# A decoder block's MLP in Strassen form: down products that share PSUM banks, and another order of the up products

## Chip, cores and metric

The kernel runs on one core of one Trainium2 chip. The metric is the device time of one execution in microseconds, the median over runs.

## What is computed

One pre-norm decoder block on 1024 tokens of width 1024, in float32. The change touches the MLP (and the last norm, which follows it); the attention part before it is left as it is.

```
v = rmsnorm(h, mlp_norm_g)
hid = square(relu(v @ w_up))        # 1024 x 4096
h = h + hid @ w_down                # 1024 x 1024
out = rmsnorm(h, final_norm_g)
```

## The kernel before

Each float32 operand of the MLP is split into a high part and a low part (`split2`: ScalarE casts the high part, VectorE or GpSimd subtracts it for the low one), and one product takes three matmuls (high x high, high x low, low x high). Both matrix products are done in 2 x 2 blocks by Strassen-Winograd: seven products in place of eight.

**Up** (lines 1188 to 1300). The 4096 columns of `w_up` are worked off in 16 quads. A quad forms blocks c11, c12, c21, c22 of the hidden values, each 128 x 512, by products named 1 to 7, of 12 matmuls of 128x512 each. `quads` writes the order by hand; TensorE's order is that of the program. For the first six quads products 1 and 2 are done earlier, and the order is (6, 5, 7, 3, 4); then it is (1, 6, 5, 7, 2, 3, 4). The last two quads run as a pair, product by product. Products and banks: 1 then 2 into `a`; 6 into `b`; 5 into `d`, and 3 on top of it; 7 into `c`, and 4 on top of it. Between them VectorE forms u2 = b + p1, u4 = d + u2 (line 1251) and c22 = c + u4 (line 1255), so product 3 enters `d` only when u4 has been read, and product 4 enters `c` only when c22 has been read. ScalarE copies p1 out of `a` before product 2 enters (line 1237). `weights(q + 1)` issues all loads, differences and splits of the next quad's weights ahead of quad q's products. After each block VectorE forms relu squared and the sums s1 to s4 that down's products want, and SyncE stores them to DRAM; the last two quads form no sums.

**Down** (line 1349 on). The 4096 rows of `w_down` are worked off in eight chunks of 512. For the first seven, `down(c)` runs seven Strassen products in the order `DORD`; each has four row blocks of 128, each block 6 matmuls (line 1395) into a PSUM tile `dn` of its own (8 tiles), and VectorE adds the tile to that product's accumulator (line 1401), seven accumulators of 128x512 by four. `prep` forms each product's operand: differences over 128x1024 in SBUF on VectorE (lines 1373, 1376, 1379, 1382) and a split. The last chunk is classical: 8 results, 192 matmuls (line 1453) after 28 combine adds of the accumulators (lines 1423 to 1429). Then come the final norm's square, mean and scale (lines 1437 to 1442) and the stores, tile by tile of 128 rows.

PSUM tiles and SBUF buffers come from pools whose next user waits for the last reader; each engine works its instructions off in order, and SyncE issues all loads and stores in order.

Of the kernel before, what the change touches and what calls it, by code (L numbers as in the profile page):

```python
# [9 lines left out]
F32 = mybir.dt.float32  # L10
# [13 lines left out]
def tile_hymba_block(  # L24
# [55 lines left out]
    def rsqrt_mean(dst, ssq, n, width, eng=None):  # L80
        m = const.tile([P, 16], F32, name="rs_mean", tag="rs_mean", bufs=3)
        (eng or nc.vector).tensor_scalar(m[:, :width], ssq, 1.0 / n, EPS, ALU.mult, ALU.add)  # L82
        nc.gpsimd.tensor_tensor(dst, m[:, :width], mhalf[:, :width], ALU.pow)  # L83
# [1024 lines left out]
    def store_hid(q, v, ap):  # L1108
        c, u = divmod(q, 2)
        if c < NQ // 2 - 1:  # L1110
            held.append((hv_dram[c][:, v, u], ap))
        elif v < V_S1 or v == V_A21:
            f_, th = {V_A11: (0, 0), V_A21: (0, 1), V_A12: (1, 0), V_A22: (1, 1)}[v]
            held.append((hl_dram[:, 2 * u + f_, th * 512:(th + 1) * 512], ap))
# [73 lines left out]
    def quad_w(q, pre):  # L1188
        raw = s8([P, ND, 2 * P], F32)
        for u in range(2):  # L1190
            nc.sync.dma_start(raw[:, u * HD:u * HD + HD],
                              w_up[u * 512:(u + 1) * 512, q * 2 * P:(q + 1) * 2 * P].rearrange("(k p) f -> p k f", p=P))
        r11, r12, r21, r22 = [raw[:, HD * d:HD * d + HD, f_ * P:f_ * P + P] for f_ in range(2) for d in range(2)]
        w = {}
        if not pre:
# [3 lines left out]
            w[V_A11], w[V_A12] = x[:, 0], x[:, 1]  # L1199
        a22 = raw_pool.tile([P, 2, HD, P], F32R, name="a22", tag="raw")  # L1200
# [11 lines left out]
        return w  # L1212

    ws_, st = {}, {}

    def weights(q):
        pre = q < NPRE
        ws_[q], st[q] = quad_w(q, pre), {}
        if pre:
            c, u = divmod(q, 2)  # L1220
            a11 = o2_tile("ho")
            nc.sync.dma_start(a11[:], hv_dram[c][:, V_A11, u])
            st[q]["p1"], st[q]["c11"] = p1_of[q][0], a11

    def quads(qs, order):
        def step(what, q):
# [6 lines left out]
            if what == 1:  # L1233
# [3 lines left out]
                nc.scalar.copy(s_["p1"][:], s_["a"][:])  # L1237
# [20 lines left out]
            elif what == 3:  # L1258
                prod(s_["d"][:], w[V_S4], B22, False, True)
                s_["c12"] = o2_tile("ho")  # L1260
                nc.vector.tensor_add(s_["c12"][:], s_["d"][:], s_["u2"][:])
                relu2(s_["c12"][:], s_["c12"][:])
                if q >= NQ - 2:
                    store_hid(q, V_A21, s_["c12"][:])
                    return
# [9 lines left out]
            else:  # L1275
# [5 lines left out]
                if q >= NQ - 2:  # L1281
# [224 lines left out]
```

## Time and profile before

| | |
|---|---|
| median of 3 runs | 1252.36 us (1252.11 to 1253.46) |
| the profiled execution | 1253.01 us |
| its span in the trace | 1251.1 us |
| busy: TensorE, VectorE | 1164.1, 954.6 us |
| busy: ScalarE, GpSimd | 531.6, 640.7 us |
| mean granted clock of TensorE | 0.982 |

The profiled execution is 1.9 us longer than its span. Busy time is that of an engine over the whole span. In the views, PE is TensorE, DVE is VectorE, ACT is ScalarE, POOL is GpSimd, SP is SyncE; a row's brackets say how long the engine stood idle before the instruction, and what it was released by.

### The profile page before, as it was taken

The page shows a single profiled execution, that of the slowest core. Times are in us where ns is not written, and L with a number is a line of the kernel's source. Part 1 is how long each engine was busy: PE and PEld are TensorE (multiplying, and loading weights), DVE is VectorE, ACT ScalarE, POOL GpSimd, SP SyncE. Part 2 cuts the span into 40 slices and gives each one's busy share as a digit, 9 for nine tenths or more (in the row PEclk, how much of TensorE's full clock was granted, in tenths as well). Part 3 has the DMA queues.
Part 4 walks back from the last instruction along what each step waited for, and adds up shares of the span by engine and source line. Part 5 has one row for each costly group of instructions (what it writes and reads, how often), then busy time and mean ns, then how long its engine had stood idle before and what let it go on. Part 6 is the DMA issues. An engine that isn't in the chain of part 4 may idle for free. (4 is left out here: it accounts for less than half of the span.)

```text
span 1251.1 us, 15875 instructions
## 1 busy us (share of the span) xinstructions
PE 1164.1 (93%) x5448; PEld 946.6 (76%) x5448; DVE 954.6 (76%) x1302; ACT 531.6 (42%) x1078; POOL 640.7 (51%) x537
## 2 busy tenths in 40 slices
PE   9998988888799999999599999999889999999997
PEld 8887766666678888887477788777668888888875
DVE  8686499999997873564878965656386899888995
ACT  6434456666766761345422222222225333334402
POOL 3433544545643361315645654545448666668652
PEclk9999999999999999999799999999989999999999
DMA  6425734342712233674336534343658434446103
GB/s 216 130 60 183 179 80 97 77 112 48 225 46 86 68 136 135 204 249 136 130 126 206 177 122 156 123 155 129 223 193 304 153 108 167 155 166 200 53 1 135
DMA packets 100288, 176.70 MB, mean 141 GB/s; under 512 B 9072, under 2 KB 53616, under 8 KB 99440
## 3 DMA queue, kind: packets, MB, share of 16 engines
q1 hardware_dynamic: 100208, 175.70, 43.8%
q8 instruction: 43, 0.70, 0.2%
q14 instruction: 37, 0.30, 0.1%
HBM read 110.13 MB, written 52.95 MB: 130 GB/s over the span
## 5 line engine op out<-in xcount | busy, mean ns | idle before, releaser
L1395 PE MATMUL dn<-s,s 128*128 128x512 f32 x1176 | 269.9, 392 | 4.6 <-DVE ho L1278 4.3
L1395 PEld LDWEIGHTS dn<-s,s 128*128 128x128 f32 x1176 | 222.2, 189 | 52.2 <-DVE ho L1278 4.7
L1076 POOL TENSOR_TENSOR s<-s,s 128x512 fp32r<-128x512 f32 x84 | 121.4, 1462 | 113.1 <-ACT s L1075 112.9
L1076 POOL TENSOR_TENSOR s<-ar,s 128x1024 fp32r<-128x1024 f32 x49 | 131.8, 2694 | 65.2 <-ACT s L1075 65.2
L1401 DVE TENSOR_TENSOR acc<-acc,dn 128x512 f32<-128x512 f32 x184 | 117.9, 677 | 31.4 <-PE dn L1395 31.3
L1075 ACT CAST s<-s 128x512 fp32r<-128x512 f32 x84 | 49.6, 619 | 177.9 <-DMA s<-in_w_up_dram 71.0
L1075 ACT CAST s<-wr 128x1024 fp32r<-128x1024 f32 x53 | 55.6, 1052 | 146.6 <-PE dn L1395 61.0
L1082 PE MATMUL pa<-b,s 128*128 128x512 f32 x384 | 97.2, 407 | 11.8 <-ACT p L1237 4.5
L1082 PEld LDWEIGHTS pa<-b,s 128*128 128x128 f32 x384 | 74.2, 196 | 30.8 <-ACT p L1237 5.7
L542 POOL TENSOR_TENSOR b<-b,w 128x512 f32<-128x512 f32 (+2 forms) x57 | 58.0, 1018 | 60.8 <-DVE w L536 41.4
L488 PE MATMUL mm<-xh,wt 128*128 128x512 f32 x256 | 87.8, 395 | 0.0
L549 PE MATMUL tr<-zid,b 128*128 128x128 f32 x288 | 52.6, 290 | 35.1 <-DVE al L557 25.1
L549 PEld LDWEIGHTS tr<-zid,b 128*128 128x128 f32 x288 | 33.5, 143 | 57.9 <-DVE al L557 43.1
L1076 DVE TENSOR_TENSOR s<-wr,s 128x1024 fp32r<-128x1024 f32 x32 | 64.8, 2024 | 6.1 <-ACT s L1075 5.6
L1076 POOL TENSOR_TENSOR s<-wr,s 128x1024 fp32r<-128x1024 f32 x21 | 51.5, 2453 | 29.4 <-ACT s L1075 29.4
L536 DVE TENSOR_TENSOR_SCAN w<-w,zid 128x129 f32<-128x129 f32 (+1 forms) x64 | 64.7, 1014 | 1.0 <-ACT w L531 0.8
L263 PE MATMUL acc<-wt,xh 128*128 128x448 f32 (+1 forms) x256 | 62.7, 379 | 1.3 <-ACT xh L214 1.3
L1082 PE MATMUL pd<-b,s 128*128 128x512 f32 x192 | 49.5, 409 | 8.3 <-DVE u L1251 4.2
L1075 ACT CAST s<-ar 128x1024 fp32r<-128x1024 f32 x49 | 51.3, 1047 | 12.5 <-DMA ar<-hv_dram 10.7
L1082 PE MATMUL pb<-t,s 128*128 128x512 f32 x192 | 49.2, 406 | 6.8 <-ACT s L1075 6.7
L488 PEld LDWEIGHTS mm<-xh,wt 128*128 128x128 f32 x256 | 48.5, 190 | 8.3 <-issue 0.2
L263 PEld LDWEIGHTS acc<-wt,xh 128*128 128x128 f32 x256 | 47.7, 188 | 9.0 <-ACT xh L214 2.0
(349 smaller groups left out, 2800.9 us busy)
## 6 DMA issues: line engine op xcount, KB each, us to landing
ar<-hv_dram SPq DMA_DIRECT2D x49, 512.0 KB, 3.7
s<-in_w_up_dram SPq DMA_DIRECT2D x32, 512.0 KB, 4.8
wr<-in_w_down_dram SPq DMA_DIRECT2D x16, 1024.0 KB, 7.1
hv_dram<-s SPq DMA_DIRECT2D x56, 256.0 KB, 2.1
hv_dram<-ho SPq DMA_DIRECT2D x42, 256.0 KB, 2.0
wr<-in_w_in_dram SPq DMA_DIRECT2D x24, 256.0 KB, 2.9
raw<-in_w_o_dram SPq DMA_DIRECT2D x8, 512.0 KB, 3.5
ht<-h_dram SPq DMA_DIRECT2D x8, 512.0 KB, 4.2
```

Of the source, the lines that this page charges most:

```text
L263: nc.tensor.matmul(accs[t][:, :width], a[:, kk, t * P:(t + 1) * P], wts[kk][:, b, :width], start=(kk == 0 and p == 0), stop=done)
L488: nc.tensor.matmul(ps[:], wt[:, a, k % 4, :], b[:, k, tsl], start=(n == 0), stop=(n == 3 * ND - 1))
L536: nc.vector.tensor_tensor_scan(rv, rv, inject, init, ALU.mult, ALU.add)
L542: eng.tensor_mul(b[:, :n], b[:, :n], w[:, 1:n + 1])
L549: nc.tensor.transpose(tr[:, j * P:(j + 1) * P], sb_a[h, Q, C, j][:, s * P:(s + 1) * P], identf[:])
L1075: nc.scalar.copy(hi, src)
L1076: eng.tensor_sub(lo, src, f(hi))
L1082: nc.tensor.matmul(ps, w[:, a, k, :], bv[:, b, k, :], start=start and n == 0, stop=n == last, skip_group_check=True)
L1395: nc.tensor.matmul(ps[:], av[:, a, u, q * P:(q + 1) * P], bv[i][:, b, u], start=(n == 0), stop=(n == 5))
L1401: nc.vector.tensor_add(dst, dst, ps[:])
```

## The change

**Down.** All eight chunks are Strassen chunks; the classical chunk and the combine adds are gone. Products 1, 6, 5 and 3 of a row block add into one PSUM bank one after the other, 7 and 4 into a second, 2 has its own. After each product the bank, as it then stands, is added to one of four result blocks (11, 21, 22, 12), which start from the residual loaded from `h_dram`. The order is (1, 2, 6, 7, 5, 4, 3). In the last chunk each result block's square, mean, scale and store follow its last add; the first column half of a tile of the upper rows is scaled by ScalarE, in the lower rows the second, after GpSimd has multiplied it by the norm's weights; the other half is scaled on VectorE. Finished tiles are held, up to two, before they are written.

```diff
-    DORD = (1, 2, 3, 5, 7, 6, 4)
+    DORD = (1, 2, 6, 7, 5, 4, 3)
...
-    acc = {i: acc_pool.tile([P, 4, 512], F32, name=f"acc{i}") for i in (1, 2, 3, 5, 7, 6, 4)}
+    acc = {k_: acc_pool.tile([P, 4, 512], F32, name=f"acc{k_}") for k_ in (11, 21, 22, 12)}
...
+    ADD_TO = {1: 11, 2: 11, 6: 21, 7: 22, 5: 22, 4: 21, 3: 12}
...
+            if i == 6:
+                nc.vector.tensor_sub(b11, b12, b11)
+                nc.vector.tensor_sub(t2[:], b22, b11)
+            elif i == 7:
+                nc.vector.tensor_sub(b12, b22, b12)
+            elif i == 4:
+                nc.vector.tensor_sub(b21, b21, t2[:])
...
+            if c == 0 and i not in DORD[:2]:
+                with tc.issue_after(st[NQ - 1]["end"].ins):
+                    prep(i)
...
-                ps = dn_ps.tile([P, 512], F32, name="dn", tag="dn")
+                if i in (1, 2, 7):
+                    banks[i, q] = dn_ps.tile([P, 512], F32, name="dn", tag="dn")
+                ps = banks[{6: 1, 5: 1, 3: 1, 4: 7}.get(i, i), q]
...
-                        nc.tensor.matmul(ps[:], av[:, a, u, q * P:(q + 1) * P], bv[i][:, b, u], start=(n == 0), stop=(n == 5))
+                        nc.tensor.matmul(ps[:], av[:, a, u, q * P:(q + 1) * P], bv[i][:, b, u],
+                                         start=i in (1, 2, 7) and n == 0, stop=n == 5, skip_group_check=True)
...
-                if c == 0 and i in (1, 5, 6):
-                    nc.scalar.copy(dst, ps[:])
-                else:
-                    nc.vector.tensor_add(dst, dst, ps[:])
+                dst = acc[ADD_TO[i]][:, q]
+                read = nc.vector.tensor_add(dst, dst, ps[:])
+                if c == NCH - 1:
+                    if i == 2:
+                        square(q, 0, dst)
+                    elif i == 5:
+                        square(4 + q, 1, dst)
+                    elif i == 4:
+                        finish(4 + q, read, square(4 + q, 0, dst))
+                    elif i == 3:
+                        finish(q, read, square(q, 1, dst))
```

**Up.** Product 3 goes to a new bank `e`, and u4 takes the place of u2 in its sum. Product 2 comes third. The next quad's weights are issued in three steps (the load; the split of `x`, which products 1 and 2 take; the rest), the last two behind the copy of product 1 for quads from the seventh on. The last two quads form s1 to s4 as all others do.

```diff
-                prod(s_["d"][:], w[V_S4], B22, False, True)
+                prod(bank("e"), w[V_S4], B22, True, True)
                 s_["c12"] = o2_tile("ho")
-                nc.vector.tensor_add(s_["c12"][:], s_["d"][:], s_["u2"][:])
+                nc.vector.tensor_add(s_["c12"][:], s_["e"][:], s_["u4"][:])
                 relu2(s_["c12"][:], s_["c12"][:])
-                if q >= NQ - 2:
-                    store_hid(q, V_A21, s_["c12"][:])
-                    return
...
-        quads([q], (6, 5, 7, 3, 4) if q < NPRE else (1, 6, 5, 7, 2, 3, 4))
-    weights(NQ - 1)
+            quads([q], (1,))
+            with tc.issue_after(st[q]["p1_ins"].ins):
+                weights(q + 1, 2)
+            quads([q], (6, 2, 5, 7, 3, 4))
+    weights(NQ - 1, 1)
     flush()
     last2 = [NQ - 2, NQ - 1]
-    quads(last2, (1, 2))
+    quads(last2[:1], (1,))
+    with tc.issue_after(st[NQ - 2]["p1_ins"].ins):
+        weights(NQ - 1, 1)
+    quads(last2[1:], (1,))
+    quads(last2, (2,))
+    with tc.issue_after(st[NQ - 1]["p1_ins"].ins):
+        weights(NQ - 1, 1)
```

How it moves instructions is shown at three places. The first is TensorE in up, one whole quad from the seventh on; a name's letter after `p` is its bank. Before:

```order
L1082 MATMUL pa_7313<-b11_5831,s8_7170 128x512 x12
L1082 MATMUL pb_7328<-t2_6380,s8_7182 128x512 x12
L1082 MATMUL pd_7343<-t1_6381,s8_7182 128x512 x12
L1082 MATMUL pc_7358<-t3_6382,s8_7183 128x512 x12
L1082 MATMUL pa_7313<-b21_5832,s8_7170 128x512 x12
L1082 MATMUL pd_7343<-b22_6383,s8_7183 128x512 x12
L1082 MATMUL pc_7358<-t4_6384,a22_7175 128x512 x12
```

With the change:

```order
L1081 MATMUL pa_7297<-b11_5831,s8_7196 128x512 x12
L1081 MATMUL pb_7334<-t2_6380,s8_7208 128x512 x12
L1081 MATMUL pa_7297<-b21_5832,s8_7196 128x512 x12
L1081 MATMUL pd_7364<-t1_6381,s8_7208 128x512 x12
L1081 MATMUL pc_7379<-t3_6382,s8_7209 128x512 x12
L1081 MATMUL pe_7395<-b22_6383,s8_7209 128x512 x12
L1081 MATMUL pc_7379<-t4_6384,a22_7201 128x512 x12
```

Product 2 (`b21`) has moved ahead of product 5 (`t1`), and product 3 (`b22`) now fills `pe` where it added into `pd`.

The second is ScalarE at the start of the last pair; `p1` is the copy of product 1, first for quad 14 and then for quad 15, `ho` the relu of product 2, and the CASTs make high parts of quad 15's weights. Before:

```order
L1075 CAST s8_8452<-s8_8449 128x512 x2
L1241 ACTIVATE ho_8408<-pa_8335 128x512
L1075 CAST a22_8457<-s8_8449 128x512
L1075 CAST s8_8464<-s8_8449 128x512
L1237 COPY p1_8494<-pa_8481 128x512
L1075 CAST s8_8464<-s8_8449 128x512
L1075 CAST s8_8465<-s8_8449 128x512 x2
L1237 COPY p1_8509<-pa_8496 128x512
L1241 ACTIVATE ho_8523<-pa_8481 128x512
L1241 ACTIVATE ho_8538<-pa_8496 128x512
```

With the change:

```order
L1238 COPY p1_8486<-pa_8473 128x512
L1074 CAST s8_8488<-s8_8463 128x512 x2
L1238 COPY p1_8506<-pa_8493 128x512
L1074 CAST a22_8538<-s8_8463 128x512
L1074 CAST s8_8545<-s8_8463 128x512
L1242 ACTIVATE ho_8520<-pa_8473 128x512
L1074 CAST s8_8545<-s8_8463 128x512
L1074 CAST s8_8546<-s8_8463 128x512 x2
L1242 ACTIVATE ho_8535<-pa_8493 128x512
```

Only casts for `x` (s8_8488) stand between the two copies now, and all casts of quad 15 stand behind the copy for quad 14.

The third is VectorE at the end of up; L1255 reads c22 of quad 14 or 15, L1261 c12, L1278 c21, and L1373 to L1382 are down's preparations. Before:

```order
L1376 TENSOR_TENSOR wr_8545<-wr_8545 128x2x512
L1117 SCALAR_TENSOR_TENSOR ho_8645<-ho_8645 128x512
L1261 TENSOR_TENSOR ho_8660<-pd_8586,u2_8569 128x512
L1117 SCALAR_TENSOR_TENSOR ho_8660<-ho_8660 128x512
L1379 TENSOR_TENSOR wr_8545<-wr_8545 128x2x512
L1261 TENSOR_TENSOR ho_8675<-pd_8601,u2_8584 128x512
L1382 TENSOR_TENSOR wr_8545<-wr_8545 128x2x512
L1117 SCALAR_TENSOR_TENSOR ho_8675<-ho_8675 128x512
L1278 TENSOR_TENSOR ho_8690<-pc_8616,u2_8569 128x512
L1117 SCALAR_TENSOR_TENSOR ho_8690<-ho_8690 128x512
L1278 TENSOR_TENSOR ho_8705<-pc_8632,u2_8584 128x512
L1117 SCALAR_TENSOR_TENSOR ho_8705<-ho_8705 128x512
```

With the change (L1262 reads c12, L1276 c21; L1265 to L1271 and L1280 form s1, s3, s2 and s4; L1412 and L1413 are down's preparations):

```order
L1262 TENSOR_TENSOR ho_8697<-pe_8684,u4_8628 128x512
L1112 SCALAR_TENSOR_TENSOR ho_8697<-ho_8697 128x512
L1265 TENSOR_TENSOR s1_8700<-ho_8697,ho_8659 128x512
L1268 TENSOR_TENSOR s3_8702<-ho_8535,ho_8697 128x512
L1271 TENSOR_TENSOR s2_8704<-s1_8700,ho_8535 128x512
L1276 TENSOR_TENSOR ho_8718<-pc_8630,u2_8583 128x512
L1112 SCALAR_TENSOR_TENSOR ho_8718<-ho_8718 128x512
L1280 TENSOR_TENSOR s4_8721<-ho_8718,s2_8682 128x512
L1276 TENSOR_TENSOR ho_8735<-pc_8646,u2_8598 128x512
L1112 SCALAR_TENSOR_TENSOR ho_8735<-ho_8735 128x512
L1280 TENSOR_TENSOR s4_8738<-ho_8735,s2_8704 128x512
L1412 TENSOR_TENSOR wr_8559<-wr_8559 128x2x512
```

The preparations of down stand behind the last read of up, and sums for quads 14 and 15 stand between the reads.

## Rows read from the trace of the kernel before

**Rows 1.** The page's busy lines: engine, busy us (share of the span), instructions.

```profile
PE 1164.1 (93%) x5448; PEld 946.6 (76%) x5448; DVE 954.6 (76%) x1302; ACT 531.6 (42%) x1078; POOL 640.7 (51%) x537
```

**Rows 2.** Windows: busy us (instructions) of PE, PEld, DVE, ACT, POOL; granted clock, DMA share, GB/s.

```profile
648.80:653.30 4.50, 4.44 (x13) 3.51 (x14) 2.19 (x2) 0.00 (x0) 3.38 (x3) 0.62 0.77 267
928.00:932.00 4.00, 3.94 (x9) 3.14 (x10) 1.99 (x4) 0.58 (x1) 0.00 (x0) 0.50 0.65 213
1038.30:1076.60 38.30, 38.30 (x171) 31.72 (x170) 32.43 (x37) 14.05 (x15) 25.12 (x10) 1.00 0.47 151
```

**Rows 3.** TensorE's waits, 640 to 1252 us: us in total, times, longest.

```profile
PE pa L1082 <- ACT p L1237: 4.5, 1, 4.5
PE dn L1395 <- DVE ho L1278: 4.3, 1, 4.3
PE pd L1082 <- DVE u L1251: 4.2, 5, 1.5
PE pd L1082 <- ACT s L1075: 4.0, 2, 2.4
PE pc L1082 <- DVE ho L1255: 1.0, 1, 1.0
PE dn L1453 <- DVE acc L1401: 0.7, 1, 0.7
```

**Rows 4.** TensorE's timeline, classical chunk: start, us, then what ran, idle before it.

```profile
1209.01 11.06 PE L1453 MATMUL dn<-s,lhr 128*128 128x512 f32 x48
```

**Rows 5.** Groups of instructions, 925 to 1200 us: busy us, mean ns.

```profile
L1401 DVE TENSOR_TENSOR acc<-acc,dn 128x512 f32<-128x512 f32 x182 | 116.6, 677 | 31.4 <-PE dn L1395 31.3
...
L1379 DVE TENSOR_TENSOR wr<-wr 128x1024 f32<-128x1024 f32 x7 | 21.6, 3090 | 5.1 <-POOL s L1076 5.1
```

**Rows 6.** VectorE's timeline at the longest wait of up.

```profile
648.04 0.68 DVE L1251 TENSOR_TENSOR u<-pd,u 128x512 f32<-128x512 f32 x1
```

**Rows 7.** TensorE's timeline at the longest wait of up.

```profile
648.86 4.59 PE L1082 MATMUL pd<-b,s 128*128 128x512 f32 x12 [2.43 <-ACT s L1075]
```

**Rows 8.** TensorE's timeline, last pair and where up meets down.

```profile
885.64 7.54 PE L1082 MATMUL pa<-b,s 128*128 128x512 f32 x24 [4.47 <-ACT p L1237]
893.02 5.75 PE L1082 MATMUL pb<-t,s 128*128 128x512 f32 x24
...
919.34 3.05 PE L1082 MATMUL pc<-t,a 128*128 128x512 f32 x12 [0.96 <-DVE ho L1255]
...
928.06 17.12 PE L1395 MATMUL dn<-s,s 128*128 128x512 f32 x64 [4.28 <-DVE ho L1278]
```

**Rows 9.** ScalarE's timeline, start of the last pair.

```profile
884.49 0.62 ACT L1075 CAST s<-s 128x512 fp32r<-128x512 f32 x1 [4.97 <-DVE s L1203]
885.01 0.58 ACT L1237 COPY p<-pa 128x512 f32<-128x512 f32 x1
```

**Rows 10.** GpSimd's timeline, start of the last pair.

```profile
880.84 1.27 POOL L1076 TENSOR_TENSOR a<-s,a 128x512 fp32r<-128x512 f32 x1
```

**Rows 11.** VectorE's timeline, in up and at the last read of up.

```profile
644.54 1.77 DVE L1284 TENSOR_TENSOR s<-ho,s 128x512 f32<-128x512 f32 x1
...
928.65 0.68 DVE L1278 TENSOR_TENSOR ho<-pc,u 128x512 f32<-128x512 f32 x1
```

**Rows 12.** VectorE's instructions by line, 909 to 927 us: busy us, mean ns.

```profile
L1373 DVE TENSOR_TENSOR wr<-wr 128x1024 f32<-128x1024 f32 x1 | 3.3, 3309 | 0.0
L1376 DVE TENSOR_TENSOR wr<-wr 128x1024 f32<-128x1024 f32 x1 | 2.8, 2802 | 0.0
...
L1379 DVE TENSOR_TENSOR wr<-wr 128x1024 f32<-128x1024 f32 x1 | 1.2, 1217 | 0.0
L1382 DVE TENSOR_TENSOR wr<-wr 128x1024 f32<-128x1024 f32 x1 | 1.2, 1211 | 0.0
```

**Rows 13.** Timeline of all engines, the end.

```profile
1240.41 1.52 PE L1453 MATMUL dn<-s,lhr 128*128 128x512 f32 x6
...
1246.77 1.42 DVE L1442 SCALAR_TENSOR_TENSOR y<-acc,fss,gfb 128x512 f32<-128x512 f32 x2 [2.03 <-POOL fss L83]
```

More of the change, by code (lines that the diff above doesn't have):

```diff
@@ L1211, in quad_w, with weights, reload_a11 @@
             w[key] = tl[:, v]
-        return w
-    ws_, st = {}, {}
-    def weights(q):
+        yield
+    ws_, st, wgen = {}, {}, {}
+    def weights(q, steps):
         pre = q < NPRE
[L1218 to L1223, printed above, removed]
+        if q not in ws_:
+            ws_[q], st[q] = {}, {}
+            wgen[q] = quad_w(q, pre, ws_[q])
+        for _ in range(steps):
+            next(wgen[q])
+    def reload_a11(q):
+        c, u = divmod(q, 2)
+        a11 = o2_tile("ho")
+        nc.sync.dma_start(a11[:], hv_dram[c][:, V_A11, u])
+        st[q]["p1"], st[q]["c11"] = p1_of[q][0], a11
     def quads(qs, order):
@@ L1280, in step @@
                 store_hid(q, V_A12, c21[:])
[L1281 to L1282 removed]
                 s4 = o2_tile("s4")
[L1284 removed]
+                s_["end"] = nc.vector.tensor_sub(s4[:], c21[:], s_["s2"][:])
                 store_hid(q, V_S4, s4[:])
@@ L1344, in load_acc, with square @@
             for q in range(4):
-                nc.sync.dma_start(acc[i][:, q], h_dram[q + rows][:, cols:cols + 512])
-        for q in range(4):
-            nc.gpsimd.tensor_sub(acc[4][:, q], acc[4][:, q], acc[7][:, q])
+                nc.sync.dma_start(acc[k_][:, q], h_dram[q + rows][:, cols:cols + 512])
+    fin = {}
+    def square(t, dh, hx):
+        sq = nc.scalar.activation(sqj[:], hx, AF.Square, accum_out=fss[t][:, dh:dh + 1])
+        fin[t, dh] = hx
+        if dh != (t < 4):
+            nc.gpsimd.tensor_mul(hx, hx, gfb[:, halves[dh]])
+        return sq
@@ new lines, in tile_hymba_block, with finish, put @@
+    ready = []
+    def finish(t, read, sq):
+        ss = fss[t]
+        nc.gpsimd.tensor_add(ss[:, 2:3], ss[:, 0:1], ss[:, 1:2])
+        rsqrt_mean(ss[:, 3:4], ss[:, 2:3], D, 1, nc.gpsimd)
+        ready.append(t)
+        with tc.issue_after(read.ins), tc.issue_after(sq.ins):
+            while len(ready) > (2 if t != 3 else 0):
+                put(ready.pop(0))
+    def put(t):
+        ss, y = fss[t], ys[t % 4]
+        for dh in ((1, 0) if t < 4 else (0, 1)):
+            sl, hx = halves[dh], fin[t, dh]
+            if dh == (t < 4):
+                nc.vector.scalar_tensor_tensor(y[:, sl], hx, ss[:, 3:4], gfb[:, sl], ALU.mult, ALU.mult)
+            else:
+                nc.scalar.activation(y[:, sl], hx, AF.Copy, scale=ss[:, 3:4])
+            if t == 3:
+                nc.sync.dma_start(out[t * P:(t + 1) * P, sl], y[:, sl])
+        if t != 3:
+            nc.sync.dma_start(out[t * P:(t + 1) * P, :], y[:])
```

126 lines of the change are left out of this document (31 added, 95 removed).

## The prediction

> **What bounds the kernel now.** I read the busy lines first: TensorE is busy 93% of the span [rows 1]. That is an average, so the next question is which stretches hold the missing 7%, and whether the change touches them. The windows of the second matrix product answer for the long steady part: TensorE is busy for all of 38.30 us at a granted clock of 1.00 while VectorE needs 32.43 [rows 2]. There only fewer matmuls help. TensorE's waits from 640 us on then give every gap [rows 3]: seven before `pd` (4.2 + 4.0 = 8.2 us), one before `pa` (4.5), one each before `pc` (1.0) and `dn` (4.3) where the two products meet, and 0.7 at the classical chunk. What lies before the up product keeps its order on every engine, so the waits before 640 us stay.
>
> **1. Fewer matmuls.** A Strassen chunk has 7 x 4 x 6 = 168 matmuls, the classical one 8 x 4 x 6 = 192; now all eight chunks have 168, so 24 go. The classical chunk ran 48 in 11.06 us [rows 4], 0.230 each, the last one's tail included: 24 x 0.230 = **-5.5 us**. Its wait of 0.7 us for an accumulator add [rows 3] goes too, as no group of blocks claims all eight banks at once any more: **-0.7**. The 28 combine adds (20 on VectorE, 8 on GpSimd) lay beside matmuls and count for nothing. VectorE's work per steady chunk stays: 28 reads and 8 operations from SBUF to SBUF. Its cover is the 38.30 - 32.43 = 5.9 us that VectorE has left [rows 2]. A bank that is used by several products must have been read before the next one enters; but there are eight banks in both kernels, one product (four blocks of 6 matmuls, 24 x 0.230 = 5.5 us) lies between a bank's use and its next use in both, and a read takes 0.677 [rows 5]. What is new is that the reads and preparations bunch differently, so that some lag is possible at eight chunk starts. The nearest row for such a lag is the 0.7 at the classical chunk [rows 3]; met once or twice in each of eight chunks it would be +6 or +11. Rows 2 show none in a steady chunk, and the slack is the same, so I allow **+1**, with 0 and +11 as ends.
>
> **2. Up: product 3 gets a bank.** Today product 3 adds into the bank `d` that product 5 filled, and must wait until VectorE has read `u4` from it. Five of the waits name that read; the other two name a cast on ScalarE, but the `u` read at line 1251 ends at 648.72 [rows 6] and TensorE goes on at 648.86 [rows 7], so they are the same wait. All seven (8.2 us) go, since product 3 now starts a bank of its own. One came with a lower clock: the window shows 0.62 [rows 2] and the product took 4.59 us in place of 2.9 (half of 5.75 for 24, [rows 8]), another 1.7. What is late next is product 4, which enters the bank `c` that c22 was read from: that read stands one VectorE instruction behind `u4`, but product 4 starts a whole product (2.9 us) after product 3. The longest of the five plain waits was 1.5 and the longest of all 2.4 [rows 3]; each plus 0.7 for the extra read is close to or below 2.9, so little is left, 0.5 by estimate. **-8.2 - 1.7 + 0.5 = -9.4**; ends: -9.9, and -2 if the wait is only handed to product 4.
>
> **3. The start of the last pair.** Product 2 of quad 14 waited 4.47 us [rows 8] for the copy of product 1, which stood behind casts of quad 15's weights on ScalarE: a cast at 884.49, then the copy at 885.01 [rows 9]. The 24 matmuls after it took 7.54 against the 5.75 of the next 24: 4.5 + 1.8 = 6.3 us. Now only quad 15's `x` split stands behind the copy for quad 14. But product 1 of quad 15 needs it: product 1(14) takes 2.9, the copy 0.58 and the first cast 0.62 [rows 9], so that with some 0.3 for the hand-overs between engines (my estimate) TensorE stands from 2.9 to about 4.4. It stands again for the first low part, 1.27 on GpSimd [rows 10], for about 0.9 more: 2.4 us of idle time: **-3.8** at full clock; ends -4.7 (only the cast is waited for) and -2.0 (1.8 for a lower clock again).
>
> **4. Where up meets down.** Before, VectorE was about 6 us behind: product 4(15) ended near 922.3 (919.34 + 3.05), its reader c21(15) ran at 928.65 [rows 8, 11]. TensorE stood 4.3 us, another 1.0 before 4(15), and ran 64 matmuls in 17.12 us [rows 8], 2.4 over 64 x 0.230, beside a clock of 0.50 [rows 2]: 7.7 us in all. Ahead of the last reads stood four preparations of down over 128x1024; they move behind the last quad: 3.31, 2.80, 1.22 and 1.21, together 8.5 us [rows 12]. New there are eight operations over 128x512 for s1, s3, s2, s4 of quads 14 and 15, since those quads now also feed Strassen products; seven of them stand ahead of the last read. At 0.68 each (the read of 128x512 in rows 11) they are 4.8, and VectorE's lag is 6.3 - 8.5 + 4.8 = 2.6 us. I add 2 for the product that follows: the loads of down's first operands come later behind the store of c11(14), and its third product's preparation (L1412, L1413, a low split) now begins only after quad 15; and 0.6 of clock. **5.2 against 7.7: -2.5.** Ends: -4.8 (the lag and 0.3 of the rest), and +8 when the seven take 1.77 each, as one of their kind did at 644.54 [rows 11] (lag 6.3 - 8.5 + 12.4 = 10.2; with the 2 for the operands, and 2.4 and 1.0 as before, 15.6).
>
> **5. The end.** Today TensorE ends near 1241.9 (1240.41 + 1.52), the last multiplication begins at 1246.77 [rows 13] and the span ends at 1251.1. After it the chain is the same in kind: add, square, mean, scale, store, with one of the last two halves on ScalarE; but results come out late and close together (first-column and second-column halves of all eight tiles in the last chunk), and up to two are held back. **+0.7**; ends -0.5 and +2.
>
> **Sum**: -5.5 - 0.7 + 1.0 - 9.4 - 3.8 - 2.5 + 0.7 = -20.2. The profiled execution took 1253.0 us, so 1232.8; the median of the runs is 0.65 lower, 1252.36, so by it **1232.2**, which I take.
>
> **The rivals.**
> (a) *VectorE becomes the pace of down; slower.* Its 32.43 us hold 28 reads x 0.677 = 19.0; eight operations share the other 13.5, 1.7 each. Were all as long as L1373's 3.31 [rows 12], VectorE would need 45.5 us per chunk, 7.2 over TensorE: 8 x 7.2 = +57, **about 1289**. It decides from a mean of 2.7 on (19.0 + 21.8 = 40.8, 2.5 over, which times eight is the whole gain). For it: L1379's mean is 3.09 [rows 5]. Against: GpSimd has no more to do than before. Chance 0.04.
> (b) *A little lag at every chunk*: the 0.7 of [rows 3] one and a half times in each, +8.4 in place of +1, **about 1239.6**. For it: each read now feeds a result block that the next read also needs, in order on one engine. Chance 0.12.
> (c) *The up wait passes to product 4* in place of vanishing: term 2 shrinks to -2, **about 1239.6**. Against: a product lies between. Chance 0.10.
> (d) *The eight new operations are blocked by GpSimd* in the handover. 128x512 out of two tiles in SBUF took 1.77 [rows 11], where reads out of PSUM take 0.68: term 4 becomes +8, **about 1242.7**. For it: GpSimd splits down's operands just then. Chance 0.12.
> The Trainium skill, "SBUF — State Buffer", section "Who interferes with whom", says that a VectorE instruction with two SBUF inputs contends with a GpSimd instruction that reads SBUF, over a port pair that is locked for the whole instruction, and that one with at most one such input does not. Rows 11 agree with that as far as they go; by it (d) would hold for each of the eight that meets a GpSimd split, and the sum would be near 1242.7; 1232.2 has them run at the length of the reads.
> (e) *The end grows* by 4, since all eight tiles come out in the last product rounds and their stores crowd: **about 1235.5**. Chance 0.05.
> (f) *The change does not do what it says*: the order of the instructions shows the new bank and the moved casts, so 0.01, 1252.
>
> **How the numbers follow.** The forecast has 0.56: its own range is 1228 to 1236. Below 1228 lie the good ends of terms 3 to 5 (0.9 + 2.3 + 1.2 = 4.4, to 1227.8). (b), (c) and (d) reach to 1242.7, two of them together to about 1250. Leaving out (a), (f) and most pairs, the range is **1227 to 1243.5**. 0.2% (2.5 us) is about what a measurement of this kernel can tell from no change. Slower by more than that needs (a): 0.03; within it are (f), a weak (a) and three rivals at once: 0.03; faster: 0.94.
>
> **What would show it.** Right: no wait before the up product's `pe`, and under 1 us before the second use of `pc`; product 1 of quad 15 waiting some 2.4 us; under 6 us idle at the first `dn`s; windows of down with TensorE full and the clock at 1.00; the last matmul some 20 us sooner. Wrong: TensorE waiting for VectorE's reads within down by more than 1 us a chunk (a, b); waits before `pc` of up (c); s1 to s4 at 1.7 us in the handover with `dn` waiting over 8 (d); more than 11 us from the last matmul to the end (e).

## The result, and the profile after

The changed kernel takes 1235.84 us (median of 4 runs, 1234.46 to 1236.29) against 1252.23 us for the kernel before: ratio 0.9866, 95% interval 0.9849 to 0.9884. That is 16.4 us faster where 20.2 were forecast (1232.2), inside the range of 1227 to 1243.5. The profiled execution took 1236.29 us with a span of 1234.5. Among the experiments' runs, one of bank_only (2187.85 us, mean clock 0.89) and one of down_only (1618.05 us, 0.65) fell into a slower state; the ratios and intervals leave them out.

TensorE's waits from 640 us on, in the trace of the changed kernel (us in total, times, longest):

```profile
PE dn L1437 <- DVE s L1075: 2.3, 1, 2.3
PE dn L1437 <- DVE ho L1276: 2.1, 1, 2.1
PE pc L1081 <- DVE ho L1256: 1.7, 2, 1.3
PE pa L1081 <- ACT s L1074: 1.2, 1, 1.2
PE pa L1081 <- POOL s L1075: 0.6, 1, 0.6
```

Against [rows 3] the seven waits before `pd` are gone, and two before the second use of `pc` have come, 1.7 us together. The start of the last pair waits 1.2 + 0.6 us where it waited 4.5, and the handover 2.3 + 2.1 where it waited 4.3 + 1.0. No wait is left inside down. TensorE's timeline at these places:

```profile
651.15 3.07 PE L1081 MATMUL pc<-t,a 128*128 128x512 f32 x12 [0.40 <-DVE ho L1256]
...
708.68 3.06 PE L1081 MATMUL pc<-t,a 128*128 128x512 f32 x12 [1.26 <-DVE ho L1256]
...
871.31 0.73 PE L1081 MATMUL pa<-b,s 128*128 128x512 f32 x2 [1.19 <-ACT s L1074]
872.66 9.62 PE L1081 MATMUL pa<-b,s 128*128 128x512 f32 x34 [0.62 <-POOL s L1075]
...
913.66 11.63 PE L1437 MATMUL dn<-s,s 128*128 128x512 f32 x43 [2.10 <-DVE ho L1276]
927.57 32.71 PE L1437 MATMUL dn<-s,s 128*128 128x512 f32 x136 [2.28 <-DVE s L1075]
```

The 34 matmuls behind the pair's wait took 9.62 us, 1.8 more than 34 x 0.230 [rows 4]. Windows over them and over the two stretches behind the waits of the handover show the granted clock, and a window over a steady stretch of down shows whether VectorE has become the pace (busy us of PE, PEld, DVE, ACT, POOL, then the clock):

```profile
872.60:882.10 9.50, 9.44 (x34) 7.62 (x35) 2.68 (x3) 2.22 (x4) 3.87 (x5) 0.82 0.00 0
914.00:928.00 14.00, 11.72 (x44) 9.27 (x43) 12.75 (x15) 5.89 (x6) 6.33 (x3) 0.87 0.94 308
928.00:932.00 4.00, 4.00 (x13) 3.11 (x13) 4.00 (x6) 0.00 (x0) 4.00 (x2) 0.63 1.05 403
1036.60:1074.90 38.30, 38.30 (x171) 31.71 (x170) 34.19 (x37) 14.03 (x14) 25.48 (x11) 1.00 0.47 151
```

The clock was 0.82 at the pair, where 1.00 was forecast, and 0.87 and 0.63 behind the two waits of the handover: means of stretches at full clock and at half, the lower of its two levels (0.50 from 873 to 876 us). In steady down TensorE is full at 1.00 as in [rows 2], with VectorE at 34.19 us of 38.30 (32.43 before), the same to 0.01 us in six such windows. The window is a little longer than a chunk: it touches 171 matmuls and not 168, and the chunks from the second on begin 38.08 us apart.

Where the time went, by stretches of the two traces (TensorE's timeline: from the span's start to the wait before the first quad's product 6, to the first matmul of the last pair, to the pair's product 6, to the first of down's second chunk, to the last of down, to the end; in the changed kernel they start at 0, 623.21, 867.22, 882.12, 956.26, 1222.98 us):

| stretch | before | after | difference | forecast |
|---|---|---|---|---|
| ahead of up's first product 6 | 621.77 | 623.21 | +1.44 | 0 |
| up to the last pair | 253.66 | 244.01 | -9.65 | -9.4 |
| products 1 and 2 of the pair | 17.59 | 14.90 | -2.69 | -3.8 |
| rest of the pair, handover, down's first chunk | 74.21 | 74.14 | -0.07 | -2.5 |
| down from its second chunk on | 274.70 | 266.72 | -7.98 | -5.2 |
| from the last matmul to the end | 9.17 | 11.52 | +2.35 | +0.7 |
| sum (span) | 1251.1 | 1234.5 | -16.6 | -20.2 |

The two rows of down make -8.05 where -7.7 was forecast, but neither does by itself. The first row is not the change's: the order of instructions there is the same in both. Over the 14 profiled executions of this study it lies between 621.25 and 624.73 us.

What made the end longer can be read in the timeline of all engines:

```profile
1210.78 2.40 POOL L1075 TENSOR_TENSOR s<-wr,s 128x1024 fp32r<-128x1024 f32 x1
...
1213.15 5.04 POOL L1368 TENSOR_TENSOR acc<-acc,gfb 128x512 f32<-128x512 f32 x4
...
1216.22 0.69 DVE L1441 TENSOR_TENSOR acc<-acc,dn 128x512 f32<-128x512 f32 x1 [0.67 <-PE dn L1437]
...
1219.29 0.75 DVE L1387 SCALAR_TENSOR_TENSOR y<-acc,fss,gfb 128x512 f32<-128x512 f32 x1 [2.39 <-POOL fss L83]
...
1219.96 0.68 DVE L1441 TENSOR_TENSOR acc<-acc,dn 128x512 f32<-128x512 f32 x1
1220.12 9.11 SPq L1393 DMA_DIRECT2D out_dram<-y  x7
```

GpSimd multiplies four halves by the norm's weights (L1368) in 5.04 us, from 1213.15, when its last split (L1075) is done. The row scale of the first finished tile stands behind that. VectorE's first scaling (L1387) waits 2.39 us for it, and the adds that read the last banks stand behind VectorE's wait: the one that should follow 1216.22 by 1.36 us comes at 1219.96. The first store is issued at 1220.12, and seven of them take SyncE 9.11 us. From the first store to the end of the span there are 14.4 us, here as in tail_split, load_one and load_four below, so that the end is as long as the first store is late. VectorE at the handover:

```profile
907.85 0.69 DVE L1265 TENSOR_TENSOR s<-ho 128x512 f32<-128x512 f32 x1
...
909.66 0.68 DVE L1262 TENSOR_TENSOR ho<-pe,u 128x512 f32<-128x512 f32 x1
...
912.92 0.68 DVE L1276 TENSOR_TENSOR ho<-pc,u 128x512 f32<-128x512 f32 x1
...
922.13 1.35 DVE L1441 TENSOR_TENSOR acc<-acc,dn 128x512 f32<-128x512 f32 x2 [0.89 <-DMA acc<-h_dram]
...
924.90 2.61 DVE L1075 TENSOR_TENSOR s<-t,s 128x1024 fp32r<-128x1024 f32 x1
```

The sums (`s`) run at 0.69 us each, between the reads of `pe` and `pc`. c21 of quad 14 is read at 912.92 only, when TensorE has stood since its first block; reads of `dn` then wait 0.89 us for their result block's load, and the low split for product 6, TensorE's second wait, comes at 924.90. GpSimd had nothing to do meanwhile:

```profile
921.67 2.42 POOL L1075 TENSOR_TENSOR s<-ar,s 128x1024 fp32r<-128x1024 f32 x1 [17.06 <-ACT s L1074]
```

### The profile page after: what moved, and what is told of

The parts are those of the page before. It is cut to its first block, busy times and chain, and to the rows that moved or that the text cites. A ratio compares the mean times of both kernels' runs of the same rounds, so it can differ in the third digit from the quotient of the medians.

```text
span 1234.5 us, 15926 instructions
## 1 busy us (share of the span) xinstructions
PE 1155.6 (94%) x5424; PEld 941.7 (76%) x5424; DVE 958.0 (78%) x1310; ACT 535.5 (43%) x1080; POOL 647.2 (52%) x539
## 5 line engine op out<-in xcount | busy, mean ns | idle before, releaser
L1437 PE MATMUL dn<-s,s 128*128 128x512 f32 x1344 | 308.6, 392 | 4.4 <-DVE s L1075 2.3
L1437 PEld LDWEIGHTS dn<-s,s 128*128 128x128 f32 x1344 | 254.4, 189 | 58.4 <-DVE s L1075 2.7
L1075 POOL TENSOR_TENSOR s<-ar,s 128x1024 fp32r<-128x1024 f32 x56 | 147.8, 2641 | 80.8 <-ACT s L1074 80.8
L1075 POOL TENSOR_TENSOR s<-s,s 128x512 fp32r<-128x512 f32 x84 | 117.0, 1414 | 109.8 <-ACT s L1074 109.8
L1441 DVE TENSOR_TENSOR acc<-acc,dn 128x512 f32<-128x512 f32 x224 | 144.0, 678 | 33.8 <-PE dn L1437 32.8
L1074 ACT CAST s<-wr 128x1024 fp32r<-128x1024 f32 x48 | 50.4, 1051 | 150.1 <-PE dn L1437 105.3
L1075 POOL TENSOR_TENSOR s<-wr,s 128x1024 fp32r<-128x1024 f32 x24 | 57.8, 2409 | 32.8 <-ACT s L1074 32.8
L1074 ACT CAST s<-ar 128x1024 fp32r<-128x1024 f32 x56 | 58.6, 1047 | 9.2 <-DMA ar<-hv_dram 9.2
L1075 DVE TENSOR_TENSOR s<-wr,s 128x1024 fp32r<-128x1024 f32 x24 | 52.4, 2182 | 6.8 <-ACT s L1074 6.8
L1112 DVE SCALAR_TENSOR_TENSOR ho<-ho 128x512 f32<-128x512 f32 x48 | 51.7, 1076 | 1.4
```

Source lines behind the costliest of these rows:

```text
L1074: nc.scalar.copy(hi, src)
L1075: eng.tensor_sub(lo, src, f(hi))
L1112: nc.vector.scalar_tensor_tensor(dst, src, 0.0, src, ALU.max, ALU.mult)
L1437: nc.tensor.matmul(ps[:], av[:, a, u, q * P:(q + 1) * P], bv[i][:, b, u], start=i in (1, 2, 7) and n == 0, stop=n == 5, skip_group_check=True)
L1441: read = nc.vector.tensor_add(dst, dst, ps[:])
```

## The experiments

Twelve kernels, in four groups, each group on its own chip beside runs of the kernel before. So the ratio to that is the number to compare; the changed kernel's is 0.9866 [0.9849, 0.9884].

| kernel | median us | ratio | interval |
|---|---|---|---|
| bank_only | 1248.27 | 0.9967 | 0.9957 to 0.9977 |
| no_bank | 1238.34 | 0.9894 | 0.9879 to 0.9909 |
| down_only | 1246.88 | 0.9955 | 0.9943 to 0.9968 |
| tail_split | 1233.49 | 0.9853 | 0.9838 to 0.9867 |
| pair_early | 1231.90 | 0.9828 | 0.9813 to 0.9842 |
| no_sums | 1229.16 | 0.9810 | 0.9794 to 0.9827 |
| load_one | 1239.51 | 0.9890 | 0.9875 to 0.9905 |
| load_four | 1263.18 | 1.0079 | 1.0064 to 1.0094 |
| old_order | 1234.17 | 0.9858 | 0.9835 to 0.9881 |
| pool_sums | 1234.84 | 0.9865 | 0.9844 to 0.9885 |
| all_three | 1231.09 | 0.9833 | 0.9818 to 0.9847 |
| loads_first | 1223.93 | 0.9763 | 0.9750 to 0.9777 |

**bank_only**, on the kernel before:

```diff
-                prod(s_["d"][:], w[V_S4], B22, False, True)
+                prod(bank("e"), w[V_S4], B22, True, True)
...
-                nc.vector.tensor_add(s_["c12"][:], s_["d"][:], s_["u2"][:])
+                nc.vector.tensor_add(s_["c12"][:], s_["e"][:], s_["u4"][:])
```

> The kernel before with one edit: product 3 of up starts a bank of its own and u4 takes the place of u2 in its sum. Everything else, the order (1, 6, 5, 7, 2, 3, 4) among it, stays. Theory (the wait was for the read of u4 out of product 3's bank): the seven waits before product 3, 8.2 us and 1.7 us of lower clock beside one of them, go; product 4 keeps at most 2 us of waits for c22. 8 to 10 us faster than before, about 1243.5. Rival (the wait is handed on to product 4, which needs the read that follows u4's): the waits before the second use of the bank c come to 6 us or more and the time falls by 3 us at most. Second rival (the new order of products does the work, not the bank): no change by the bank alone.

Measured: 0.33% faster, some 4 us: half of the theory's 8 to 10, and neither rival. TensorE's timeline shows why:

```profile
650.56 3.06 PE L1082 MATMUL pc<-t,a 128*128 128x512 f32 x12 [0.36 <-DVE ho L1255]
...
799.42 3.01 PE L1082 MATMUL pa<-b,s 128*128 128x512 f32 x12 [0.75 <-ACT p L1237]
...
861.08 3.01 PE L1082 MATMUL pa<-b,s 128*128 128x512 f32 x12 [0.99 <-ACT p L1237]
```

No product 3 waits, and product 4 waits 0.36 us in one quad of the first six. But in four later quads product 2 now waits 0.58 to 0.99 us for ScalarE's copy of product 1, which stands behind a cast for the next quad:

```profile
798.26 0.62 ACT L1075 CAST s<-s 128x512 fp32r<-128x512 f32 x1 [5.01 <-DVE s L1203]
798.78 0.58 ACT L1237 COPY p<-pa 128x512 f32<-128x512 f32 x1
```

The trace of before has no such wait; as I read it, the quads were held up at product 3 first. Up to the last pair it takes 246.59 us by its trace, 7.1 less than before, and products 1 and 2 of the pair take 19.57 us, 2.0 more: 1.0 of that are new waits at the pair's start. The bank removes all seven waits, but it uncovers the copy.

**no_bank**, the reverse edit on the changed kernel.

> The changed kernel with product 3 of up back on product 5's bank (and u2 in its sum); the new order of the products stays. Theory: the waits for u4 come back, 7 to 10 us slower than the changed kernel, about 1244.5. Rival (the new order, which puts product 2 earlier, has removed the waits): no more than 2 us slower.

Measured: ratio 0.9894 against 0.9866, 2.5 us by the medians; the intervals touch. By the trace, up to the last pair takes 248.81 us, 4.8 more than in the changed kernel, nearly all of it in two of the first six quads:

```profile
649.95 4.58 PE L1081 MATMUL pd<-b,s 128*128 128x512 f32 x12 [2.51 <-DVE u L1252]
...
710.21 3.04 PE L1081 MATMUL pd<-b,s 128*128 128x512 f32 x12 [1.92 <-DVE u L1252]
```

The run's time shows less of it, in part because the pair's lower clock stayed away here, 1.6 us (see the last section). From the seventh quad on no product 3 waits, although it adds into product 5's bank. In the first six, where the next quad's splits are issued behind product 6, the waits come back. So my term 2 came out by two causes: the bank removed the two long waits of the first six quads, and for the five short ones the reordered and split work was enough by itself.

**old_order** undoes only the place of product 2:

```diff
-            quads([q], (6, 2, 5, 7, 3, 4))
+            quads([q], (6, 5, 7, 2, 3, 4))
```

> The changed kernel with the old order of products (1, 6, 5, 7, 2, 3, 4) for the quads from the seventh on; product 3's own bank and the weights in steps behind the copy of product 1 stay. Theory, as it now stands: from the seventh quad on any of two things ends the waits for u4 (a bank of its own, or two products between 5 and 3 together with the casts behind the copy), and with the bank alone the copy of product 1 was the next thing late, since casts stood ahead of it; with the casts behind the copy the old order has no wait, so no change, within 2 us. Rival (the order itself is needed): waits of 0.6 to 1 us before product 2 in four or five quads, or before product 3, 3 us or more slower.

Measured: 0.9858 [0.9835, 0.9881], no change, and its trace has no wait before product 2. With the bank there, the new order of the products adds nothing that can be measured; what bank_only lacked is that the casts stand behind the copy of product 1.

**down_only** puts up back as a whole (product 3 on bank `d`, the old order, `weights(q + 1, 3)` ahead of each quad, `quads(last2, (1, 2))`) and keeps down and the sums.

> The changed kernel with up as before: product 3 on product 5's bank, the old order, each quad's weights issued in one piece ahead of the quad before it, both products 1 of the last pair behind all casts of quad 15. What is left of the change is down, its end and the sums of the last two quads. Theory: up costs 9.7 us more and the start of the last pair 2.7 us more than in the changed kernel, so about 1248, 4 us faster than before: 24 matmuls (-5.5) and the classical chunk's wait (-0.7) and 1 at the handover, less 2.3 for the longer end. Rival (the equal chunks alone make most of the gain): 1242 or less. Rival (down alone costs, its gain being eaten by the end and the handover): 1252 or more.

Measured: 0.9955, 5.7 us faster by the medians; 4 were expected.

```profile
885.59 8.55 PE L1081 MATMUL pa<-b,s 128*128 128x512 f32 x24 [4.53 <-ACT p L1238]
...
925.17 8.68 PE L1423 MATMUL dn<-s,s 128*128 128x512 f32 x37 [0.31 <-DVE ho L1276]
...
937.01 23.21 PE L1423 MATMUL dn<-s,s 128*128 128x512 f32 x89 [3.15 <-DVE s L1075]
```

The pair's wait for the copy is back at 4.53 us. Down, from its first matmul to its last, takes 311.60 us against 319.71, and the end is 11.53 us, as in the changed kernel. The 8.1 us were not won at the handover: the first chunk takes 44.88 us (45.01 before), and from the second chunk on there are 266.72 us, as in the changed kernel, against 274.70. At the pace of a steady chunk, 168 matmuls in 38.08 us, the 24 matmuls are 5.4 of these 8.0; the classical chunk lost another 1.6 (it takes 45.31 us, the changed kernel's last one 38.24), and two of the seven chunks before it 0.9 (38.35 and 38.71 us). The end gives 2.4 back. What the changed kernel has beyond this, 11 us by the ratios, is up: -9.8 up to the last pair and -3.7 in its products 1 and 2 by the traces, +1.4 in down's first chunk, and +1.6 ahead of up, where nothing differs.

**tail_split**, on the changed kernel:

```diff
-                        5: (b11, nc.vector), 4: (b21, nc.gpsimd), 3: (b22, nc.gpsimd)}[i]
+                        5: (b11, nc.vector), 4: (b21, nc.gpsimd),
+                        3: (b22, nc.vector if c == NCH - 1 else nc.gpsimd)}[i]
```

> The changed kernel with one edit: in the last chunk the low part of product 3's operand is subtracted on VectorE and not on GpSimd. Theory: the end is 2.3 us longer than before because GpSimd reaches its four multiplications by the norm's weights (5.04 us) and the first row scale behind them only after that split, VectorE waits 2.39 us for that scale with the reads of the last product behind it; with 2.4 us of split gone from GpSimd the scales come 2.4 us earlier, the wait goes, and the time falls by 1.5 to 2.5 us, to about 1234. Rival (the end is bound by 4 MB of stores that move at some 390 GB/s from their first issue): it gains the same only if the first store moves as early; if the first store is issued as late as now, no change. Rival (VectorE is late with the split itself): TensorE waits before product 3 of the last chunk, up to 2 us slower.

Measured: 0.9853; its interval and the changed kernel's overlap, so the ratio alone doesn't show the gain. By its trace the end takes 10.14 us after the last matmul in place of 11.52:

```profile
1209.97 5.05 POOL L1368 TENSOR_TENSOR acc<-acc,gfb 128x512 f32<-128x512 f32 x4
...
1216.93 9.11 SPq L1393 DMA_DIRECT2D out_dram<-y  x7
```

The multiplications begin at 1209.97, 11.19 us ahead of its last matmul's end (1221.16); in the changed kernel 1213.15 is 9.83 us ahead of 1222.98. They come 1.36 us earlier, and the end is 1.38 us shorter. The first store goes out 4.2 us ahead of the last matmul's end and not 2.9. The 2.4 us of the theory did not come in full: GpSimd's other split for product 3 took 3.40 us there, beside VectorE's, in place of 2.40.

**pair_early**, on the changed kernel:

```diff
+    weights(NQ - 1, 1)
     quads(last2[:1], (1,))
-    with tc.issue_after(st[NQ - 2]["p1_ins"].ins):
-        weights(NQ - 1, 1)
     quads(last2[1:], (1,))
```

> The changed kernel with one edit: the split of quad 15's x is issued before product 1 of quad 14 and not behind its copy; all other casts of quad 15 stay behind the copies. Theory: TensorE stands 1.19 and 0.62 us at the start of the last pair because product 1 of quad 15 waits for casts behind that copy, and the next 34 matmuls take 1.9 us too long at a clock of 0.82; with the split done early there is no wait, the clock stays at 1.00, and the pair starts 3.7 us faster, about 1232. Rival (the lower clock there does not come from the wait): only 1.8 us faster, 1234. Rival (the early casts delay the copy of product 1, as before the change): a wait of 2 us or more before product 2 of quad 14, no gain.

Measured: 0.9828, 0.38% below the changed kernel's ratio, 4 to 5 us.

```profile
867.06 11.06 PE L1081 MATMUL pa<-b,s 128*128 128x512 f32 x48
877.96 5.79 PE L1081 MATMUL pb<-t,s 128*128 128x512 f32 x24
```

Products 1 and 2 of the pair, 48 matmuls, take 10.90 us without a wait (14.90 in the changed kernel), and the clock stays at 1.00. The trouble before the change was that the copy stood behind casts of quad 15's sums and differences, for which ScalarE stood 4.97 us [rows 9]; the casts for `x` alone, ahead of it, delay nothing.

**no_sums**, on the changed kernel: in the last two quads `store_hid(q, v, s_["c12"][:])` for each of the four sums, and no sum formed; down's first differences follow the last relu of c21.

> The changed kernel with the eight sums s1 to s4 of quads 14 and 15 left out; c12 is stored in their places, so down's last chunk multiplies other values. Theory (VectorE's lag at the handover is made by these eight operations, 0.68 us each, 5.4 in all): the wait of 2.10 us for c21 goes, and the wait of 2.28 for the low part of product 6's operand shrinks or goes, since that part is formed 5.4 us earlier: 3 to 6 us faster than the changed kernel, about 1231.5. Rival (the wait for product 6 hangs on the loads of the result blocks or on the order of the reads, not on VectorE's lag): at most 2 us faster. Rival (GpSimd blocks these sums): they would take 1.7 us each in the changed kernel; its trace already shows 0.68, so nothing is expected of this.

Measured: 0.9810, 7 us below the changed kernel by ratio. Down's only wait is

```profile
927.72 262.55 PE L1443 MATMUL dn<-s,s 128*128 128x512 f32 x1157 [1.13 <-POOL s L1075]
```

and the low split for product 6 is

```profile
919.54 1.22 DVE L1075 TENSOR_TENSOR s<-t,s 128x1024 fp32r<-128x1024 f32 x1
```

Down takes 306.64 us from its first matmul to its last, 6.3 less than in the changed kernel; all of it is in the first chunk (39.92 us against 46.24, where a steady one takes 38.08). So most of the handover's loss in the changed kernel, waits and lower clock, comes from these eight operations of 0.69 us, by VectorE's order or by the stores that wait for them. Part of it is indirect: the split above took 2.61 us in the changed kernel, beside one that GpSimd began at 924.05. Another 1.6 of the 7 us is the pair's clock, which was not lowered in this run. The sums run at full speed in the changed kernel; rival (d) did not occur, since GpSimd stood idle for 17.06 us just there.

**load_one** and **load_four**, on the changed kernel, with `LOADS = (7,)` and `LOADS = (2, 7, 5, 3)`:

```diff
+            if i in LOADS:
+                nc.vector.tensor_sub(xtra[:], wr[:, 0], wr[:, 1])
```

> The changed kernel with one more VectorE operation in each chunk of down: the difference of two rows of 128x1024 in SBUF, written to a tile that nobody reads. Theory (TensorE paces down, VectorE has 38.30 - 34.19 = 4.1 us to spare per chunk): 1.2 to 3.3 us fit into that, no change, within 2 us. Rival (reads out of the shared banks have no slack, so that any delay of VectorE's shows): 1.2 us or more in each of eight chunks, 10 us slower or more.

> The changed kernel with four more such VectorE operations in each chunk of down, spread over products 2, 7, 5 and 3. Theory: 34.19 + 4 x 1.2 to 4 x 2.4 = 39 to 44 us per chunk against 38.3, so VectorE paces down: 5 to 45 us slower, 1241 to 1281. Rival (they fit, since the steady chunk's VectorE time holds much waiting for GpSimd that would move): under 3 us slower. It prices how near VectorE is to being the pace.

Measured: 0.9890 and 1.0079, 3 us and 27 us slower. A window of about one chunk of each, load_one first:

```profile
1036.60:1074.90 38.30, 38.30 (x171) 31.72 (x170) 35.17 (x38) 14.05 (x14) 25.77 (x11) 1.00 0.46 151
```

```profile
1057.50:1098.90 41.40, 39.27 (x168) 31.20 (x168) 41.40 (x41) 14.04 (x14) 29.21 (x11) 1.00 0.42 139
```

With one more operation TensorE stays full (VectorE at 35.17 of 38.30), and down from its second chunk on takes 266.72 us, the same as in the changed kernel: reads out of shared banks have slack. The 3 us come from elsewhere. The first chunk takes 1.5 us more, the pair's clock, not lowered in this run, gives 1.6 back, and the end is 14.3 us long, 2.8 more than in the changed kernel:

```profile
1216.14 5.04 POOL L1370 TENSOR_TENSOR acc<-acc,gfb 128x512 f32<-128x512 f32 x4
...
1222.27 0.75 DVE L1389 SCALAR_TENSOR_TENSOR y<-acc,fss,gfb 128x512 f32<-128x512 f32 x1 [5.14 <-POOL fss L83]
```

GpSimd's multiplications begin 7.06 us ahead of the last matmul's end (1223.20), 2.77 later than the 9.83 of the changed kernel, and VectorE's first scaling waits 5.14 us for the scale behind them. In load_four they begin 6.3 us ahead, 3.5 later, and the end is 15.0 us, 3.5 more. With tail_split this makes four points on one line: the end moves by what the multiplications move. With four more operations VectorE is busy for all of the 41.40 us, and the chunks begin some 41.4 us apart in place of 38.08: 3.4 us in each, 27 in eight. So what rival (a) describes begins at some 4 us more of VectorE time per chunk, and the changed kernel stays short of it.

**pool_sums**, on the changed kernel: `se = nc.gpsimd if q >= NQ - 2 else nc.vector` forms s1 to s4, and down's first differences follow the last relu of c21.

> The changed kernel with the eight sums s1 to s4 of quads 14 and 15 formed on GpSimd, which stands idle for 17 us at that place; down's first differences are issued behind the last relu of c21. Nothing is left out. Theory (the handover's waits come from these eight operations standing ahead of other work on VectorE): both waits, 2.10 and 2.28, go as where the sums were left out, 4 to 6.5 us faster than the changed kernel, about 1230.5. Rival (VectorE's operations from SBUF to SBUF, the relus and L1412, L1413, are held up by GpSimd's, and GpSimd's next splits come late): at most 2 us faster, with VectorE's 128x512 relus at 1.5 us or more.

Measured: 0.9865, no change. It is the rival's number without the rival's reason. The wait for c21 is gone; TensorE, VectorE and SyncE show the new one:

```profile
926.46 0.76 PE L1438 MATMUL dn<-s,s 128*128 128x512 f32 x1 [3.57 <-DVE acc L1442]
```

```profile
912.73 1.05 DVE L1278 SCALAR_TENSOR_TENSOR ho<-ho 128x512 f32<-128x512 f32 x1
...
915.41 2.31 DVE L1413 TENSOR_TENSOR wr<-wr 128x1024 f32<-128x1024 f32 x1
...
925.63 1.34 DVE L1442 TENSOR_TENSOR acc<-acc,dn 128x512 f32<-128x512 f32 x2 [5.69 <-DMA acc<-h_dram]
```

```profile
910.30 8.89 SPq L1105 DMA_DIRECT2D hv_dram<-s  x6
...
921.53 0.88 SPq L1361 DMA_DIRECT2D acc<-h_dram  x2
```

Beside GpSimd's sums VectorE's relus take 1.05 us in place of 0.69, and the difference over 128x1024 (L1413) 2.31, where it takes 1.22 in the changed kernel with GpSimd idle. The Trainium skill, "SBUF — State Buffer", section "Who interferes with whom", says that a VectorE instruction with two inputs in SBUF contends with a GpSimd instruction that reads SBUF; these rows agree. That loss is small here. But VectorE's first read of `dn` stands 5.69 us for the loads of the result block. SyncE issues these from 921.53 on, behind the stores of the sums, six of which hold it for 8.89 us. The sums had two followers, VectorE's reads and SyncE's queue; only one was freed.

**all_three** joins tail_split, pair_early and pool_sums.

> The changed kernel with three edits together: product 3's split of the last chunk on VectorE (2.3 us faster alone), quad 15's x split ahead of product 1 of quad 14 (4 us faster alone), and the sums of quads 14 and 15 on GpSimd (4 to 6.5 expected). They lie in three places, so they should add: 10 to 13 us faster than the changed kernel, about 1224. Rival (a lower clock that one of them removed shows up at another wait, so they don't add): 1228 or more.

Measured: 0.9833, some 4 us below the changed kernel and not the 10 to 13 us that were hoped for: no better than pair_early alone. The rival's number came, not its reason: what pool_sums paid at the handover by itself is here too, a wait of 3.70 us for VectorE's reads and a granted clock of 0.51 from 921 to 928 us, so that it adds nothing.

**loads_first**, on all_three: the stores of the last two quads are issued behind the first result block's loads.

```diff
-    flush()
...
-                nc.sync.dma_start(acc[k_][:, q], h_dram[q + rows][:, cols:cols + 512])
+                ld = nc.sync.dma_start(acc[k_][:, q], h_dram[q + rows][:, cols:cols + 512])
+            if k_ == 11:
+                with tc.issue_after(ld.ins):
+                    flush()
```

> The kernel all_three with one more edit: the loads of the first result block are issued on SyncE ahead of the stores of quads 14 and 15 (the stores are put behind them); the loads of the other three stay behind those stores. Theory: with the sums on GpSimd, the wait at the handover is no longer for VectorE's sums but for these loads, which stand behind stores that wait for the sums (VectorE stood 5.69 us for them, TensorE 3.57 us for VectorE's first reads); with the loads ahead, the first reads run as the products end, both waits (3.70 and 0.93 in all_three) shrink to 1.5 us at most, and the time falls by 3 to 5 us to about 1227. Rival (the sums' contention with VectorE's preparations is what is late, not the loads): no more than 1 us faster. Rival (the other result blocks, now the latest loads, take over the wait): a wait for the second read of a bank, before product 7 or 5, of 2 us or more.

Measured: 0.9763 [0.9750, 0.9777], 1223.93 us: 29 us faster than the kernel before on its chip, and some 12 to 13 faster than the changed kernel. TensorE's waits from 640 us on are down to

```profile
PE pc L1081 <- DVE ho L1256: 1.8, 2, 1.3
PE dn L1440 <- DVE s L1075: 1.5, 1, 1.5
```

The waits did what the theory said: the one for VectorE's reads is gone, the other is 1.5 us. The gain over all_three is 8 to 9 us by the ratios where 3 to 5 were expected; by the traces down's first chunk takes 40.02 us against 47.24, since the lower clock behind the waits, which the theory had not counted, is gone too (1.00 from 880 to 960 us). This version beats both kernels.

## Why the prediction was right, and where it was off

The time came out inside the range, 3.6 us above the forecast. Part of that nearness is luck: the two largest misses, terms 1 and 4, have opposite signs.

**Term 1 (fewer matmuls, steady down): right in kind, and too small, -7.98 for -5.2.** TensorE is full in a steady chunk, no wait stands in down after the handover, and rival (b) did not occur. The 24 matmuls gave 5.4 us as forecast; the allowance of +1 for bunched reads was not needed; and the kernel before lost 2.5 us in its classical chunk and two others where I had counted the 0.7 of the one wait that I looked at. One reading of mine was wrong without harm: I took VectorE's slack in a chunk to stay at 5.9 us, and it fell to 4.1, with as many operations. load_one shows that this is still enough, load_four where it ends.

**Term 2 (up): right in size, -9.65 against -9.4, wrong in part as to the cause.** I put all seven waits on the bank. bank_only and no_bank show that the bank answers for the two long ones, and that alone it hands the five short ones on to the copy of product 1, which had not been late in the trace of before. Rival (c)'s follower is late, but little: product 4 waits 1.7 us, not 6; the estimate was 0.5. That is 1.2 more than I allowed, and the stretch is still as short as forecast, by another 1.4 us that no named wait accounts for.

**Term 3 (the last pair): the idle time was over-, the clock under-estimated.** 2.4 us of idle were forecast, 1.81 came (the 0.3 that I had allowed for hand-overs between engines is not in the first wait: 1.19, with 0.58 + 0.62 for the copy and the cast). But "at full clock" failed: 0.82, another 2.2 us (14.90 - 10.90 of pair_early - 1.81). The end of the range that I had given for it, -2.0, was nearer to the -2.7 than the value that I took.

**Term 4 (the handover): right in kind, and its gain did not come, -0.07 for -2.5.** VectorE's lag was the wait, the sums ran at 0.69 us as assumed, and the two waits, 2.10 + 2.28, are what I had counted (2.6 + 2). What I had wrong is the clock behind them: 0.6 us by the forecast, some 3.3 by the windows above (14.00 us at 0.87 and 4.00 at 0.63). In no_sums, where 1.13 us of waiting is left, the first chunk is 1.8 us longer than a steady one; in the changed kernel it is 8.2.

**Term 5 (the end): +2.35 for +0.7.** I counted the chain per tile and two held tiles, and left out GpSimd: four multiplications, 5.04 us together, that the scale of the first finished row stands behind. tail_split, load_one and load_four move the end by moving GpSimd's work, -1.4, +2.8 and +3.5 us; with it 1.4 us earlier the end is 1.0 longer than before, near the 0.7. The sign that I had given for rival (e) came, 11.52 us for the limit of 11, but not its 4 us, and not for its reason: the stores move as a whole with the first one.

The remaining 1.44 us of the 3.6 that are missing lie ahead of up, where nothing was changed.

## What to carry to other kernels

When a wait is removed, ask of every reader of the same engine what had been waiting unseen behind it: here the bank freed product 3 and uncovered a copy behind casts, and the freed sums uncovered loads behind stores in SyncE's queue. Work that is new at the seam of two stages costs its full length there and more (eight times 0.69 us, 5.5, and the loss that they made was 6.3), while one more operation in every steady chunk vanished in VectorE's slack of 4 us. A wait has to be priced with the lower clock that can follow it: at the handover that was some 3.3 us beside 4.4 of waiting. In the last chunk count the in-order work of every engine, also of the one that is idle half of the time on average.

## What was not expected of the hardware

The lower clock after a wait comes or stays away where the instructions around it are the same. Behind the same waits of 1.19 and 0.62 us at the start of the last pair, the next 34 matmuls took 9.62 us in the changed kernel and in pool_sums, 9.58 in tail_split and 9.60 in load_four, but 8.04 in no_bank, 8.01 in no_sums, 7.98 in load_one, and in old_order

```profile
871.87 8.00 PE L1081 MATMUL pa<-b,s 128*128 128x512 f32 x34 [0.62 <-POOL s L1075]
```

So this wait has two prices, 1.6 us apart, each paid by four of eight kernels, and no run tells which will be paid. What decides between them stays open. It is as large as many of the differences that were sought, and with the spread of 3.5 us ahead of up it is why a single profiled execution places a term within a us or two, and not better.
